# A decoder layer on one core: the last six pieces of the last gate through GpSimd's queue, the router bias beside the second output block

## The chip, the cores and the metric

The kernel runs on one core of a Trainium2 chip. The metric is the device time of one execution in microseconds (us). A core has TensorE (PE; its weight loads are PEld), VectorE (DVE), ScalarE (ACT) and GpSimd (POOL); SyncE (SP) here does little else than issue transfers. One set of 16 DMA engines moves all data between device memory and the core's own memory. An instruction stream runs strictly in its order on each engine, and an engine that waits holds up all that is behind it in its stream.

## The reference

The layer takes 256 tokens of width 2048, in float32. What matters here:

```python
ada = jax.nn.silu(c) @ w_ada[l] + b_ada[l]
sh1, sc1, gt1, sh2, sc2, gt2 = jnp.split(ada, 6, axis=-1)
h = modulate(rmsnorm(x, norm1_g[l]), sh1, sc1)
...                                              # input projection, attention, pooling
x = x + gt1[:, None, :] * (mix @ w_out[l])
h2 = modulate(rmsnorm(x, norm2_g[l]), sh2, sc2)
x = x + gt2[:, None, :] * hier_moe(h2, w_grp[l], w_exp[l], w1[l], w3[l], w2[l])
```

`hier_moe` picks one of 4 groups by the logits of `w_grp`, two of its 8 experts by those of `w_exp`, and adds the two experts' SwiGLU outputs, `(silu(h2 @ w1[e]) * (h2 @ w3[e])) @ w2[e]`, by their weights. The 32 experts' weights are 12 MB each and are all read.

## The kernel before

Three stages follow each other: the input projection with the vectors of the first sub-layer; attention, pooling and the output projection; the experts. Tile's scheduler decides at build time in which order each engine's instructions stand.

**Gates.** The vectors `gt1, sc2, sh2, gt2` are sums over 16 pieces of `w_ada` each. `ada_pieces` loads a piece (128x2048, 1 MB) into a slot through SP's queue (L177) and adds it, times `sT`, to an accumulator on VectorE (L178). `gt2` is section 5, the last; its accumulator lies in G6. From the second output projection on, the slots are the two halves of buffer G4 (tile `g4_70`) and buffer B8 (tiles `w_1976`, `w_1983` and so on), in turn. When all 16 pieces are in, `gate_end` sums over partitions by four products with `ones` (L290), each of which waits for the copy of the one ahead on ScalarE (L291).

**Second output projection and router.** `out_proj(mixA, ...)` (L613 products; L617, L618 on VectorE) goes through four blocks of 512 columns; its weights lie in G2 (`g2_68`) and G3 (`g3_69`). After each, `route_block` turns the block (L679, copies L681 and L682), forms router products (L686) with `h` in G7, sums squares (L690) and copies x for the gather (L693). `route_bias` (L670, 16 products, and the copy L672 into `brt`) stands after the third block. Then VectorE makes logits (L697, L708), the group and the two experts (L720 to L737), `memf`; products with `tri` and `ones` (L741 to L745) count tokens per expert; `pos` (L747) and the slot matrix `gq` (L784, L786) follow. `weights()` makes the combine weights `cmb`, and `most`, `mosti` (L767, L768), which SP loads into a register (L971) for the rare overflow path.

**Experts.** They go in eight quarters of 4 experts with 32 token slots each. `gather` builds `xg`: 64 products' worth of `x1c` by `gq` (L796), two groups of eight scalings (L800), a turn of the weights (L803) and its copy (L805). `hidden` goes through two halves of 1024 rows; in each, it takes the four `w1` tiles and then the four `w3` tiles of the quarter, 32 products each (L820); every tile is 2 MB (L815). A product shows as two records in the trace. All four tiles of such a block are read in turn, row group by row group, so each is free only near the block's end. `down` takes eight `w2` tiles (L856). Tiles go round a ring of buffers, G5, G1, G2, G3, G0, G7, G4, to which G6 comes when `gt2` is done. So the first `w3` block of the first quarter lies in G0, G7, G4 and G5 (second use), and the second half's `w1` in G1, G2, G3 and G0 (second use).

Of the kernel before, what the change touches and what calls it, by code (L numbers as in the profile page):

```python
# [12 lines left out]
ALU = mybir.AluOpType  # L13
AX = mybir.AxisListType.X
PSUM = bass.MemoryType.PSUM

P = 128
D = 2048
NT = 2
# [13 lines left out]
NE = 32  # L33
DE = 512
CAP = 32
RB = 8
RR = 4
QE = 4
# [41 lines left out]
def layer_kernel(ctx: ExitStack, tc: tile.TileContext, x, c, w_ada, b_ada, norm1_g, w_in, q_norm_g,  # L80
                 k_norm_g, w_pool, pool_scale, w_out, norm2_g, w_grp, w_exp, w1, w3, w2,
                 kconst, kband, out):
    nc = tc.nc
    x, out = x[0], out[0]
    w_ada, b_ada, w_in, w_out = w_ada[0], b_ada[0], w_in[0], w_out[0]
# [35 lines left out]
    def slot(shape, ring, key):  # L121
        t, at = turn(ring, key)
        if at is None:
            return one.tile(shape, F32, tag=t, name="w")
        return piece_of(t, at, shape)

    def bank(shape, tag):
        return ps1.tile(shape, F32, tag=tag, name=tag, bufs={"mm": 2, "sm": 1, "fl": 1}[tag])

    def banks(shape):  # L130
        return ps2.tile(shape, F32, tag="b2", name="b2")

    def t2(shape=(P, 512)):
        return rot.tile(list(shape), F32, tag="t2", name="t2", bufs=4)

    def r4(shape):
        return piece_of("G7", turn((0, 1024, 2048), "r4"), shape)
# [23 lines left out]
    ones = one.tile([P, P], F32, name="ones")  # L161
# [9 lines left out]
    nc.vector.tensor_copy(sT, pt[:, 0:16])  # L171


    def ada_pieces(sec, acc):
        def piece(k):
            w = slot([P, D], *fill_ring)
            nc.sync.dma_start(w, w_ada[k * P:(k + 1) * P, sec * D:(sec + 1) * D])  # L177
            nc.vector.scalar_tensor_tensor(acc, w, sT[:, k:k + 1], acc, op0=ALU.mult, op1=ALU.add)  # L178

        return [lambda k=k: piece(k) for k in range(KC)]  # L180
# [83 lines left out]
    for kq in range(4):  # L264
        pt = banks([P, 4, S])
        for i in range(NT):
            for j in range(4):
                k = kq * 4 + j
# [68 lines left out]
    def fill(n):  # L337
        for _ in range(n):
            step = next(steps, None)
            if step is not None:  # L340
                step()
                nsteps[0] += 1
# [331 lines left out]
    def route_block(n):  # L674
        xv = xs[:, :, n * 512:(n + 1) * 512].rearrange("p i (q r) -> p i r q", q=P, r=RR)
        pt = banks([P, 4, S])
        for i in range(NT):
            for u in range(4):
                nc.tensor.transpose(pt[:, u, i * P:(i + 1) * P], xv[:, i, u], ident)  # L679
        h = r4([P, 4, S])  # L680
        nc.scalar.copy(h[:, 0:2], pt[:, 0:2])  # L681
        nc.vector.tensor_copy(h[:, 2:4], pt[:, 2:4])  # L682
        pl = bank([P, NT, 36], "sm")
        for i in range(NT):
            for u in range(4):
                nc.tensor.matmul(pl[:, i], lhsT=h[:, u, i * P:(i + 1) * P], rhs=ws2[:, n * 4 + u],  # L686
                                 start=(u == 0), stop=(u == 3))
        for i in range(NT):
            t = t2()
            nc.scalar.activation(t, xs[:, i, n * 512:(n + 1) * 512], AF.Square, accum_out=ss2[:, i, n:n + 1])  # L690
        for i in range(NT):
            xc = xs[:, i, n * 512:(n + 1) * 512].rearrange("p (q r) -> p r q", r=RB)
            nc.scalar.copy(x1c[i][:, n // 2, :, (n % 2) * 64:(n % 2 + 1) * 64], xc)  # L693
        if n == 0:
            nc.vector.tensor_copy(lr, pl)
        else:
            nc.vector.tensor_add(lr, lr, pl)  # L697
        if n < 2:
            fill(9)
        if n == 2:  # L700
            route_bias()

    out_proj(mixA, 0, "wo_attn", route_block)
# [6 lines left out]
    def small(name, *shape):  # L710
        return one.tile([P, NT, *shape], F32, name=name)

    def bc(ap, *shape):
        return ap.to_broadcast([P, NT, *shape])
# [21 lines left out]
    memf = small("mem", NE)  # L736
    nc.vector.tensor_scalar(memf, lz, THRESH, None, op0=ALU.is_lt)  # L737


    pr = bank([P, 3, NE], "sm")  # L740
    nc.tensor.matmul(pr[:, 0], lhsT=tri, rhs=memf[:, 0], start=True, stop=True)  # L741
    nc.tensor.matmul(pr[:, 1], lhsT=ones, rhs=memf[:, 0], start=True, stop=False)
    nc.tensor.matmul(pr[:, 1], lhsT=tri, rhs=memf[:, 1], start=False, stop=True)
    nc.tensor.matmul(pr[:, 2], lhsT=ones, rhs=memf[:, 0], start=True, stop=False)
    nc.tensor.matmul(pr[:, 2], lhsT=ones, rhs=memf[:, 1], start=False, stop=True)  # L745
    pos = small("pos", NE)
    nc.vector.scalar_tensor_tensor(pos, pr[:, 0:2], 1.0, memf, op0=ALU.add, op1=ALU.mult)  # L747

    cmb, over = small("cmb", NE), small("over", NE)
    most = one.tile([P, 1], F32, name="most")  # L750
    mosti = one.tile([P, 1], I32, name="mosti")

    def weights():

        eg, sg, se = small("eg", NG), small("sg", 1), small("se", 1)
        nc.vector.tensor_sub(eg, lg, bc(mg, NG))
        nc.vector.tensor_sub(cmb, lm, bc(l8[:, :, 0:1], NE))
        nc.scalar.activation(eg, eg, AF.Exp)
        nc.scalar.activation(cmb, cmb, AF.Exp)
        nc.vector.tensor_mul(cmb, cmb, memf)  # L760
        nc.vector.reduce_sum(sg, eg, axis=AX)
        nc.vector.reduce_sum(se, cmb, axis=AX)
        nc.vector.tensor_mul(sg, sg, se)
        nc.vector.reciprocal(sg, sg)
        nc.vector.tensor_mul(cmb, cmb, bc(sg, NE))
        nc.vector.scalar_tensor_tensor(over, pr[:, 0:2], float(CAP), cmb, op0=ALU.is_ge, op1=ALU.mult)
        nc.vector.reduce_max(most, pr[:, 2], axis=AX)  # L767
        nc.vector.tensor_copy(mosti, most)  # L768


# [10 lines left out]
    def gather(e0):  # L781
        gq = rot.tile([P, NT, QE, CAP], F32, tag="gq", name="gq")
        gw = t2([P, NT, QE, CAP])
        nc.vector.tensor_tensor(gw, bc(iota[:, None, None, :], QE, CAP), bc(pos[:, :, e0:e0 + QE, None], QE, CAP), op=ALU.is_equal)  # L784
        for i in range(NT):
            nc.vector.tensor_scalar(gq[:, i], gw[:, i], rs2[:, i:i + 1], None, op0=ALU.mult)  # L786
        if e0 == 0:
            weights()
        nc.vector.tensor_mul(gw, gw, bc(cmb[:, :, e0:e0 + QE, None], QE, CAP))
        xg = one.tile([P, KC, QS], F32, tag="B8" if e0 // QE % 2 else "Pi", name="xg")  # L790
        for kq in range(2):
            px = banks([P, 8, QS])
            for u in range(8):
                k = kq * 8 + u
                for i in range(NT):
                    nc.tensor.matmul(px[:, u], lhsT=x1c[i][:, k // RB, k % RB],  # L796
                                     rhs=gq[:, i].rearrange("p e s -> p (e s)"), start=(i == 0), stop=(i == NT - 1))
            for u in range(8):
                k = kq * 8 + u
                nc.vector.tensor_scalar(xg[:, k], px[:, u], sc2T[:, k:k + 1], sh2T[:, k:k + 1], op0=ALU.mult, op1=ALU.add)  # L800
        pt = bank([P, NT, P], "sm")
        for i in range(NT):
            nc.tensor.transpose(pt[:, i], gw[:, i].rearrange("p e s -> p (e s)"), ident)  # L803
        gwT = rot.tile([P, NT, P], F32, tag="gwT", name="gwT")
        nc.vector.tensor_copy(gwT, pt)  # L805
        return xg, gwT
# [198 lines left out]
```

## Time and profile before

| | us |
|---|---|
| three runs | 1395.58, 1395.92, 1398.74 |
| median | 1395.92 |
| the profiled execution | 1393.28 |
| its span, first to last instruction | 1391.5 |
| TensorE busy | 1071.9 (77%) |
| VectorE busy | 447.1 (32%) |
| ScalarE busy | 100.0 (7%) |
| SP's queue (q1), share of 16 DMA engines' span | 97.9% |
| moved by DMA | 557.27 MB, mean 400 GB/s |

The profiled execution's own time is 1.78 us over its span. All times below count from the span's start. A row of a timeline gives start, length, engine, line, operation, output and inputs, count and, in brackets, how long the engine had been idle and what ended that. The granted clock is a share of 2.4 GHz.

### The profile page before, as it was taken

What the parts mean: (1) busy time and instruction counts of PE and PEld (TensorE: products, weight loads), DVE (VectorE), ACT (ScalarE), POOL (GpSimd) and SP (SyncE); (2) the same over time, 40 slices, a digit from 0 to 9 for tenths busy, and PEclk for the clock granted to TensorE, in tenths of its full rate; (3) what the DMA queues carried; (4) which work ended last, traced back from release to release, by engine and by line L of the source; (5) the groups of instructions that cost most, each with busy time, mean ns of one, the idle gap of its engine ahead of it and who ended that gap; (6) DMA issues with size and microseconds to landing.
All of it is one profiled execution on the core that took longest, in us unless ns stands there. A gap on an engine that the chain in (4) does not pass through costs nothing.

```text
span 1391.5 us, 12491 instructions
## 1 busy us (share of the span) xinstructions
PE 1071.9 (77%) x5227; PEld 433.6 (31%) x5227; DVE 447.1 (32%) x725; ACT 100.0 (7%) x225; POOL 9.1 (1%) x11
## 2 busy tenths in 40 slices
PE   4899998998997776677758767676776766777566
PEld 2455654544456231122213113121321311222112
DVE  1196667999677210201202111020220202012002
ACT  3200000424222000000000000000000000000000
POOL 1000000000000000000000000000000000000000
PEclk9999999999997979879979988997998998898789
DMA  9999998999999799999999999999999999999997
GB/s 320 328 385 385 400 386 324 342 361 322 400 365 405 325 427 428 427 428 427 427 429 428 428 429 426 427 428 428 428 429 427 428 427 427 428 429 428 429 424 283
DMA packets 101259, 557.27 MB, mean 400 GB/s; under 512 B 18792, under 2 KB 31056, under 8 KB 68688
## 3 DMA queue, kind: packets, MB, share of 16 engines
q1 hardware_dynamic: 97664, 554.22, 97.9%
q10 hardware_dynamic: 3472, 2.20, 0.5%
q8 instruction: 43, 0.70, 0.2%
q14 instruction: 16, 0.13, 0.0%
q0 software_dynamic: 64, 0.02, 0.0%
HBM read 554.31 MB, written 2.10 MB: 400 GB/s over the span
## 4 chain that ended last, share of the span: by engine, by line
DMA 52%; PE 33%; DVE 9%; issue 3%; SPq 2%; ACT 1%; ACTq 0%; DVEq 0%
DMA w<-in_w_dram 49%; PE mm L820 11%; PE mm L475 5%; PE mm L613 5%; PE b L861 4%; PE b L485 3%; DVE g L178 3%; DMA g<-in_w_in_dram 2%; DMA g<-in_w_ada_dram 1%; PE b L877 1%; DVE bacc L219 1%; SPq L815 1%; PE b L796 1%; DVE g L408 1%; DMA v8T<-in_b_ada_dram 1%
## 5 line engine op out<-in xcount | busy, mean ns | idle before, releaser
L820 PE MATMUL mm<-w,xg 128*32 128x512 f32 x2048 | 341.9, 704 | 162.8 <-DMA w<-in_w_dram 162.8
L861 PE MATMUL b<-w,t 128*32 128x512 f32 x896 | 178.0, 671 | 86.5 <-DMA w<-in_w_dram 81.0
L820 PEld LDWEIGHTS mm<-w,xg 128*32 128x32 f32 x2048 | 76.9, 126 | 415.1 <-DMA w<-in_w_dram 229.0
L800 DVE TENSOR_SCALAR xg<-b,sc2T,sh2T 128x128 f32<-128x128 f32 x128 | 42.3, 404 | 390.8 <-PE b L796 390.8
L475 PE MATMUL mm<-g,hT 128*128 128x512 f32 (+1 forms) x320 | 127.6, 553 | 12.0 <-DMA g<-in_w_in_dram 7.1
L178 DVE SCALAR_TENSOR_TENSOR g<-g,sT,g 128x2048 f32<-128x2048 f32 x52 | 122.0, 2346 | 12.2 <-DMA g<-in_w_ada_dram 12.1
L613 PE MATMUL mm<-g,mix 128*128 128x512 f32 x256 | 114.8, 601 | 4.2 <-DVE t L617 4.2
L861 PEld LDWEIGHTS b<-w,t 128*32 128x32 f32 x896 | 41.9, 116 | 217.6 <-DMA w<-in_w_dram 120.5
L841 DVE TENSOR_TENSOR t<-b,gt 128x512 f32<-128x512 f32 (+1 forms) x33 | 20.9, 671 | 273.0 <-PE b L861 250.7
L475 PEld LDWEIGHTS mm<-g,hT 128*128 128x128 f32 x320 | 57.2, 199 | 78.3 <-issue 64.2
L613 PEld LDWEIGHTS mm<-g,mix 128*128 128x128 f32 x256 | 48.2, 193 | 60.7 <-issue 55.1
L844 PE MATMUL mm<-t,gwT 128*128 128x512 f32 (+1 forms) x132 | 62.6, 605 | 3.3 <-DVE t L841 2.8
L796 PEld LDWEIGHTS b<-gq,x1c 128*128 128x128 f32 x512 | 59.8, 196 | 13.1 <-issue 6.7
L796 PE MATMUL b<-gq,x1c 128*128 128x128 f32 x512 | 62.7, 282 | 1.2 <-DVE gq L786 1.2
L824 ACT ACTIVATE t<-mm 128x512 f32<-128x512 f32 x8 | 4.8, 597 | 816.7 <-PE mm L820 816.7
L485 PE MATMUL b<-hT,g 128*128 128x256 f32 x256 | 56.9, 380 | 0.5 <-DMA g<-in_w_in_dram 0.4
L485 PEld LDWEIGHTS b<-hT,g 128*128 128x128 f32 x256 | 48.4, 190 | 11.2 <-issue 3.2
L846 DVE TENSOR_TENSOR xs<-xs,mm 128x512 f32<-128x512 f32 (+1 forms) x66 | 44.3, 671 | 17.7 <-PE mm L844 17.5
L825 DVE TENSOR_TENSOR t<-t,mm 128x512 f32<-128x512 f32 x8 | 5.5, 688 | 116.3 <-PE mm L820 116.3
L219 DVE SCALAR_TENSOR_TENSOR bacc<-g,sT,bacc 128x1024 f32<-128x1024 f32 x28 | 35.9, 1283 | 7.1 <-DMA g<-in_w_ada_dram 4.6
L844 PEld LDWEIGHTS mm<-t,gwT 128*128 128x128 f32 x132 | 21.2, 188 | 45.2 <-DVE xs L846 28.4
L178 DVE SCALAR_TENSOR_TENSOR g<-w,sT,g 128x2048 f32<-128x2048 f32 x12 | 28.1, 2346 | 2.3 <-DMA w<-in_w_ada_dram 2.2
(208 smaller groups left out, 514.4 us busy)
## 6 DMA issues: line engine op xcount, KB each, us to landing
w<-in_w_dram SPq DMA_DIRECT2D x190, 2048.0 KB, 21.3
g<-in_w_ada_dram SPq DMA_DIRECT2D x52, 1024.0 KB, 8.3
g<-in_w_ada_dram SPq DMA_DIRECT2D x44, 512.0 KB, 9.5
g<-in_w_in_dram SPq DMA_DIRECT2D x21, 1024.0 KB, 10.9
g<-in_w_out_dram SPq DMA_DIRECT2D x16, 1024.0 KB, 9.5
w<-in_w_ada_dram SPq DMA_DIRECT2D x12, 1024.0 KB, 7.4
w<-in_w_ada_dram SPq DMA_DIRECT2D x20, 512.0 KB, 9.7
g<-in_w_in_dram SPq DMA_DIRECT2D x14, 512.0 KB, 8.7
```

What stands on the lines that cost most here:

```text
L178: nc.vector.scalar_tensor_tensor(acc, w, sT[:, k:k + 1], acc, op0=ALU.mult, op1=ALU.add)
L219: nc.vector.scalar_tensor_tensor(acc, w[:, kk], sT[:, k:k + 1], acc, op0=ALU.mult, op1=ALU.add)
L475: nc.tensor.matmul(po[:, :width], lhsT=hcols(k0 + j, slice(i * P, (i + 1) * P)), rhs=w[:, j], start=(j == 0), stop=(j == nk - 1))
L485: nc.tensor.matmul(ppool[n][:, u], lhsT=w[:, j, u * P:(u + 1) * P], rhs=hcols(k, slice(0, S)), start=(k == 0 and u % 2 == 0), stop=(k == K ...
L613: nc.tensor.matmul(po, lhsT=mix[:, k, i * P:(i + 1) * P], rhs=ws[k // 4][:, k % 4], start=(k == 0), stop=(k == 7))
L796: nc.tensor.matmul(px[:, u], lhsT=x1c[i][:, k // RB, k % RB], rhs=gq[:, i].rearrange("p e s -> p (e s)"), start=(i == 0), stop=(i == NT - 1))
L800: nc.vector.tensor_scalar(xg[:, k], px[:, u], sc2T[:, k:k + 1], sh2T[:, k:k + 1], op0=ALU.mult, op1=ALU.add)
L820: nc.tensor.matmul(h[e * CAP:(e + 1) * CAP, :], lhsT=xg[:, k, e * CAP:(e + 1) * CAP], rhs=ws[e][:, r], start=(k == 0), stop=(k == KC - 1), ...
L841: nc.vector.tensor_mul(y[:, 0:m], py, gt2[:, c0:c0 + m])
L844: nc.tensor.matmul(pz[:, 0:m], lhsT=gwT[:, i], rhs=y[:, 0:m], start=True, stop=True)
L846: nc.vector.tensor_add(xv, xv, pz[:, 0:m])
L861: nc.tensor.matmul(py[n // 2][e * CAP:(e + 1) * CAP, (n % 2) * 512:(n % 2 + 1) * 512], lhsT=aT[:, f, e * CAP:(e + 1) * CAP], rhs=ws[e][:, ...
```

## The change

`gather(0)` puts a column of the first slot matrix `gq` on a list, `behind`. From then on a gate piece is loaded through GpSimd's queue, and ahead of each load VectorE copies that column into the piece's slot (L183), so that the load stands after it. At that point ten of the sixteen pieces of `gt2` have been made, and six are left. `route_bias` is called after the second block, not after the third. The two products for `most` (L744, L745 before) get a tile of their own and are formed in `weights()`, which with the product `gw * cmb` moves behind the gather's products in the program.

```diff
+    behind = []
     def ada_pieces(sec, acc):
         def piece(k):
             w = slot([P, D], *fill_ring)
-            nc.sync.dma_start(w, w_ada[k * P:(k + 1) * P, sec * D:(sec + 1) * D])
+            if not behind:
+                nc.sync.dma_start(w, w_ada[k * P:(k + 1) * P, sec * D:(sec + 1) * D])
+            else:
+                nc.vector.tensor_copy(w[:, 0:1], behind[0])
+                nc.gpsimd.dma_start(w, w_ada[k * P:(k + 1) * P, sec * D:(sec + 1) * D])
             nc.vector.scalar_tensor_tensor(acc, w, sT[:, k:k + 1], acc, op0=ALU.mult, op1=ALU.add)
...
-        if n == 2:
+        if n == 1:
             route_bias()
...
-    pr = bank([P, 3, NE], "sm")
+    pr = bank([P, NT, NE], "sm")
...
-    nc.tensor.matmul(pr[:, 2], lhsT=ones, rhs=memf[:, 0], start=True, stop=False)
-    nc.tensor.matmul(pr[:, 2], lhsT=ones, rhs=memf[:, 1], start=False, stop=True)
...
-        nc.vector.reduce_max(most, pr[:, 2], axis=AX)
+        pm = bank([P, NE], "fl")
+        nc.tensor.matmul(pm, lhsT=ones, rhs=memf[:, 0], start=True, stop=False)
+        nc.tensor.matmul(pm, lhsT=ones, rhs=memf[:, 1], start=False, stop=True)
+        nc.vector.reduce_max(most, pm, axis=AX)
...
         if e0 == 0:
-            weights()
-        nc.vector.tensor_mul(gw, gw, bc(cmb[:, :, e0:e0 + QE, None], QE, CAP))
+            behind.append(gq[:, 1, 0, 0:1])
...
+        if e0 == 0:
+            weights()
+        nc.vector.tensor_mul(gw, gw, bc(cmb[:, :, e0:e0 + QE, None], QE, CAP))
```

SP's stream at the start of the experts. Here `w_1998` and `w_1996` are the first half's last two `w1` tiles, `w_2032` to `w_2038` the first half's `w3` tiles of experts 0 to 3 (G0, G7, G4, G5), `w_2072` to `w_2076` the second half's `w1` tiles of experts 0 to 2 (G1, G2, G3), `w_2078` the one of expert 3 (G0), `w_2285` a `w2` tile in G6. Before:

```order
L177 DMA g4_70<-in_w_ada_dram 128x2048
L815 DMA w_2034<-in_w3_dram 128x4096
L177 DMA g4_70<-in_w_ada_dram 128x2048
L971 TENSOR_LOAD mosti_1897
L971 ISA x2
L815 DMA w_2036<-in_w3_dram 128x4096
L815 DMA w_2038<-in_w3_dram 128x4096
L815 DMA w_2072<-in_w1_dram 128x4096
L815 DMA w_2074<-in_w1_dram 128x4096
L815 DMA w_2076<-in_w1_dram 128x4096
L856 DMA w_2285<-in_w2_dram 128x4096
L815 DMA w_2078<-in_w1_dram 128x4096
```

The same place in SP's stream of the change, where 7 is added to most numbers: `w_2039`, `w_2041`, `w_2043`, `w_2045` are the first half's `w3` tiles of experts 0 to 3 (`w_2043` is the one in G4), `w_2079` to `w_2083` and `w_2085` the second half's `w1` tiles, `w_2292` the `w2` tile in G6:

```order
L825 DMA w_2041<-in_w3_dram 128x4096
L981 TENSOR_LOAD mosti_1895
L981 ISA x2
L825 DMA w_2045<-in_w3_dram 128x4096
L825 DMA w_2079<-in_w1_dram 128x4096
L825 DMA w_2081<-in_w1_dram 128x4096
L825 DMA w_2083<-in_w1_dram 128x4096
L825 DMA w_2043<-in_w3_dram 128x4096
L825 DMA w_2085<-in_w1_dram 128x4096
L825 DMA w_2119<-in_w3_dram 128x4096
L825 DMA w_2121<-in_w3_dram 128x4096
L825 DMA w_2123<-in_w3_dram 128x4096
```

The six gate pieces are gone from SP's stream, the load into G4 stood first of five behind the register load and now stands fifth, and the load into G6 stood sixth and now comes after the last row shown.

TensorE's stream where the first `w3` block begins (in the change, after the whole first `w1` block). `fl` tiles are the gate's final sums. Before:

```order
L820 MATMUL mm_1991<-w_2034,xg_1920 32x512
L290 MATMUL fl_2156<-g6_72,ones_94 128x512
L290 MATMUL fl_2159<-g6_72,ones_94 128x512
L290 MATMUL fl_2162<-g6_72,ones_94 128x512
L290 MATMUL fl_2165<-g6_72,ones_94 128x512
L820 MATMUL mm_1991<-w_2036,xg_1920 32x512
L820 MATMUL mm_1991<-w_2038,xg_1920 32x512
L820 MATMUL mm_1991<-w_2032,xg_1920 32x512
```

The same place in the change:

```order
L830 MATMUL mm_1998<-w_2039,xg_1901 32x512
L830 MATMUL mm_1998<-w_2041,xg_1901 32x512
L830 MATMUL mm_1997<-w_2079,xg_1901 32x512
L830 MATMUL mm_1997<-w_2081,xg_1901 32x512
L830 MATMUL mm_1997<-w_2083,xg_1901 32x512
L297 MATMUL fl_2163<-g6_72,ones_94 128x512
L297 MATMUL fl_2166<-g6_72,ones_94 128x512
L297 MATMUL fl_2169<-g6_72,ones_94 128x512
L830 MATMUL mm_1998<-w_2043,xg_1901 32x512
L830 MATMUL mm_1998<-w_2045,xg_1901 32x512
L830 MATMUL mm_1998<-w_2039,xg_1901 32x512
L830 MATMUL mm_1998<-w_2041,xg_1901 32x512
```

One product of each second-half `w1` tile and three of the gate's sums now stand ahead of the first product with `w_2043`; 30 of the block's 32 products stand behind that, and the last read of `w_2039`, whose buffer G0 the load of `w_2085` needs, is the 25th of them.

VectorE's stream from the slot matrix on, in the change (before, the six L178 rows stood one by one from the third output block on, and two of them between the router's steps):

```order
L794 TENSOR_SCALAR gq_1896<-t2_1897,rs2_1857 128x128 x2
L775 TENSOR_REDUCE most_1894<-fl_1966 128x1
L810 TENSOR_TENSOR t2_1897<-t2_1897,cmb_1892 128x256
L183 COPY w_1977<-gq_1896 128x1
L776 CAST mosti_1895<-most_1894 128x1
L183 COPY g4_70<-gq_1896 128x1 x2
L807 TENSOR_SCALAR xg_1901<-b2_1902,sc2T_1478,sh2T_1651 128x128 x8
L185 SCALAR_TENSOR_TENSOR g6_72<-w_1977,sT_102,g6_72 128x2048
L807 TENSOR_SCALAR xg_1901<-b2_1927,sc2T_1478,sh2T_1651 128x128 x8
L815 COPY gwT_1975<-sm_1972 128x256
L183 COPY w_1987<-gq_1896 128x1
L185 SCALAR_TENSOR_TENSOR g6_72<-g4_70,sT_102,g6_72 128x2048 x2
```

All six piece products stand behind the first group of scalings, and the last three pieces' copies come only after slots have been read.

## Rows read from the trace of the kernel before

**Rows 1.** Page, the chain that ended last, by line.

```profile
DMA w<-in_w_dram 49%; PE mm L820 11%; PE mm L475 5%; PE mm L613 5%; PE b L861 4%; PE b L485 3%; DVE g L178 3%; DMA g<-in_w_in_dram 2%; DMA g<-in_w_ada_dram 1%; PE b L877 1%; DVE bacc L219 1%; SPq L815 1%; PE b L796 1%; DVE g L408 1%; DMA v8T<-in_b_ada_dram 1%
```

**Rows 2.** Stretches: length, busy by engine, TensorE's granted clock, DMA share, GB/s.

```profile
429.00:440.00 11.00, 6.85 (x32) 6.59 (x31) 6.15 (x19) 2.43 (x4) 0.00 (x0) 0.50 1.01 430
...
452.60:460.60 8.00, 8.00 (x75) 3.72 (x75) 7.26 (x17) 0.00 (x0) 0.00 (x0) 1.00 0.05 20
462.00:470.00 8.00, 5.97 (x14) 1.33 (x10) 0.00 (x0) 2.34 (x4) 0.00 (x0) 1.00 0.99 422
500.00:1350.00 850.00, 610.34 (x3412) 187.97 (x3404) 113.06 (x242) 6.06 (x9) 0.00 (x0) 0.86 1.01 428
```

**Rows 3.** Timeline of SP's queue, 420 to 515 us.

```profile
441.02 0.33 SPq L177 DMA_DIRECT2D g<-in_w_ada_dram  x1
459.79 4.89 SPq L815 DMA_DIRECT2D w<-in_w_dram  x5
```

**Rows 4.** Line L815 from 455 to 470 us: five loads, issue to landing.

```profile
DMA to landing us min/median/max: 7.9/18.3/24.8
```

**Rows 5.** Timeline of VectorE, 425 to 460 us.

```profile
428.46 0.69 DVE L682 COPY g<-b 128x512 f32<-128x512 f32 x1 [1.11 <-ACT g L681]
...
451.18 2.64 DVE L800 TENSOR_SCALAR xg<-b,sc2T,sh2T 128x128 f32<-128x128 f32 x8 [0.37 <-PE b L796]
...
457.09 0.42 DVE L805 COPY gwT<-sm 128x256 f32<-128x256 f32 x1
457.42 2.35 DVE L178 SCALAR_TENSOR_TENSOR g<-g,sT,g 128x2048 f32<-128x2048 f32 x1
```

**Rows 6.** The chain in order of time: start, length, what; 422 to 446 us.

```profile
423.19 2.34 DVE g L178
425.53 0.61 DVE xs L618
...
432.64 3.61 PE sm L686 x16
...
438.75 2.25 DVE g L178
...
443.50 0.43 PE sm L744 x2
...
444.75 0.10 DVE most L767
```

**Rows 7.** Timeline of TensorE, 409 to 436 us.

```profile
411.13 1.42 PE L686 MATMUL sm<-ws,g 128*128 128x36 f32 x12
...
416.37 6.17 PE L613 MATMUL mm<-g,mix 128*128 128x512 f32 x14
...
426.77 5.48 PE L670 MATMUL sm<-wr,sh2T 128*128 128x36 f32 x32
```

**Rows 8.** Timeline of TensorE, 445 to 526 us.

```profile
445.56 8.94 PE L796 MATMUL b<-gq,x1c 128*128 128x128 f32 x64 [1.20 <-DVE gq L786]
...
454.64 7.94 PE L820 MATMUL mm<-w,xg 128*32 128x512 f32 x68
462.51 1.13 PE L290 MATMUL fl<-g,ones 128*128 128x512 f32 x2
464.31 1.12 PE L290 MATMUL fl<-g,ones 128*128 128x512 f32 x2 [0.68 <-ACT gt L291]
...
472.65 8.76 PE L820 MATMUL mm<-w,xg 128*32 128x512 f32 x60 [2.63 <-DMA w<-in_w_dram]
...
498.66 9.39 PE L820 MATMUL mm<-w,xg 128*32 128x512 f32 x60 [7.88 <-DMA w<-in_w_dram]
...
518.23 7.05 PE L820 MATMUL mm<-w,xg 128*32 128x512 f32 x58 [0.47 <-DMA w<-in_w_dram]
```

**Rows 9.** GpSimd's timeline, and VectorE's, at 333 us.

```profile
333.44 2.34 DVE L178 SCALAR_TENSOR_TENSOR g<-g,sT,g 128x2048 f32<-128x2048 f32 x1
...
333.70 0.49 POOL L283 DMA_DIRECT2D g<-in_b_ada_dram  x1 [0.30 <-POOL g L281]
```

More of the change, by code (lines that the diff above doesn't have):

```diff
@@ L743, in layer_kernel @@
     nc.tensor.matmul(pr[:, 1], lhsT=tri, rhs=memf[:, 1], start=False, stop=True)
-    nc.tensor.matmul(pr[:, 2], lhsT=ones, rhs=memf[:, 0], start=True, stop=False)
-    nc.tensor.matmul(pr[:, 2], lhsT=ones, rhs=memf[:, 1], start=False, stop=True)
     pos = small("pos", NE)
-    nc.vector.scalar_tensor_tensor(pos, pr[:, 0:2], 1.0, memf, op0=ALU.add, op1=ALU.mult)
+    nc.vector.scalar_tensor_tensor(pos, pr, 1.0, memf, op0=ALU.add, op1=ALU.mult)
     cmb, over = small("cmb", NE), small("over", NE)
@@ L765, in weights @@
         nc.vector.tensor_mul(cmb, cmb, bc(sg, NE))
-        nc.vector.scalar_tensor_tensor(over, pr[:, 0:2], float(CAP), cmb, op0=ALU.is_ge, op1=ALU.mult)
-        nc.vector.reduce_max(most, pr[:, 2], axis=AX)
+        nc.vector.scalar_tensor_tensor(over, pr, float(CAP), cmb, op0=ALU.is_ge, op1=ALU.mult)
+        pm = bank([P, NE], "fl")
+        nc.tensor.matmul(pm, lhsT=ones, rhs=memf[:, 0], start=True, stop=False)
+        nc.tensor.matmul(pm, lhsT=ones, rhs=memf[:, 1], start=False, stop=True)
+        nc.vector.reduce_max(most, pm, axis=AX)
         nc.vector.tensor_copy(mosti, most)
```

## The prediction

> **What bounds the kernel now.** I read the chain that ended last first: half of it is waiting for weight transfers [rows 1]. The stretches say how hard the DMA engines work: from 500 to 1350 us they move 428 GB/s without a pause [rows 2]. At that rate a 2 MB weight tile takes 4.9 us and a 1 MB gate piece 2.45 us, and whatever the engines compute in the expert stage is hidden behind it. So the time is set by how many bytes are in when the expert stage begins, that is, by how long the DMA engines stand still around 410 to 500 us. They do in one place: 452.6 to 460.6 us, share 0.05 [rows 2]. SP's queue says why: after the last gate piece (441.02) nothing is issued until 459.79 [rows 3]. The load that stands next in SP's stream goes into G4, which the last piece product on VectorE, 457.42 to 459.77 [rows 5], still reads. Five loads then go out, the first lands 7.9 us later [rows 4], of which 4.9 are its bytes and 3.0 the way there and the notice; and from 462 us on the transfers never stop again [rows 2]. TensorE goes on in the first `w3` block at 472.65 and, after the seventh load, at 498.66 [rows 8]. That last row is my mark: the six loads ahead had landed 4.9 us earlier, at 493.8.
>
> **The change part by part.** *The way to the slot matrix gets shorter.* On it now stand a piece product between the two-expert search and its next step, 2.25 us; the two pairs of `most` products, 0.43 each; and the `most` reduction, 0.10 [rows 6]. All leave it: 3.2 us. The router bias moves into the last dense block. Its 32 records took 5.48 us; twelve records of like products between dense ones took 1.42, or 0.119 each [rows 7], so there it costs 32 x 0.119 = 3.8 us. The dense products, which ended at 416.37 + 6.17 = 422.5 [rows 7], end at 426.3. No piece product (2.34 us) now stands between the two VectorE steps of 0.6 to 0.7 us that follow [rows 6], so x is done at 427.7, where it was at 426.1 [rows 6]. From there to the end of the second copy took 428.46 + 0.69 - 426.14 = 3.0 us [rows 5, 6]; the eight router products of the block before, now ahead, add some 0.3: 431.0. The last 16 records take 1.9 us at 0.119 or 3.6 as measured [rows 6], so they end at 432.9 to 434.6; they ended at 436.2. Gain 1.6 to 3.3; I take 2.4. Together 5.6 us, bounds 4.8 to 6.5: the gather, which began at 445.56 [rows 8], begins at 440.0.
>
> *The first block.* From the gather's start to the first expert product it was 9.1 us, and 68 records took 7.94 [rows 8]. The 64 records of the first `w1` block thus run from 449.1 to 456.6; its tiles are last read in its last four products, about 0.7 us from the end. At 455.9 SP's four reloads go out; the register load ahead of them waits for `mosti`, which is ready soon after the gather starts, so it costs nothing. Their bytes begin some 1.4 us later, at 457.3 (half of the 3.0).
>
> *The gate pieces.* SP no longer carries them. The idle stretch moves rather than goes: pieces one to three are issued at about 441 and are through by 451. Piece four needs a slot back. The first scalings start 451.18 - 445.56 = 5.6 us after the gather [rows 5, 8]; scalings 2.64, piece product 2.35, scalings 2.64, and a copy of about 0.4 [rows 5] follow: issued at 453.7, through at about 457.6. Pieces five and six come two piece products later, at 458.5, with the reloads. The six slot copies are one column each and cost nothing beside those. What GpSimd needs to issue 1 MB is in no row: 0.33 us is SP's issue [rows 3], 0.49 GpSimd's for 8 KB [rows 9]. I take 0.5; the lower end changes nothing, and the upper end is the length of one VectorE instruction, 2.35 us, by which piece four would fall among the reloads: +2.45.
>
> The row at 333.70 shows GpSimd's issue done in 0.49 us while a piece product of 2.34 us ran on VectorE [rows 9]. The Trainium skill, SBUF — State Buffer, "SBUF: two separate sides", has a rule against this change: GpSimd cannot write the descriptors of its transfers while VectorE runs a two-port operation such as a float32 copy, and the transfer waits for its end. By the row, 0.5 us stands; by the rule the sum would be 2.45 higher, if a two-port operation lay there. No run here shows one beside a large transfer of this queue.
>
> *The load into G4 comes last.* This is the term that decides. In SP's stream four reloads stand ahead of it. Bytes from 457.3: four reloads 19.6, pieces five and six 4.9, a rest of piece four 0.3, and its own 4.9 make 487.0; it lands 1.6 later, at 488.6. (It must be in the queue by 481. If both queues share the engines, piece six lands near 472, and its product ends by 476.) Before, G4 came first, the block began when the second of five had landed, and three loads, 14.7 us, were under way meanwhile. Now all seven buffers are full when it lands, and SP's next load, into G0, waits for a block that has hardly begun. The load into G6, which filled that place before, stands behind it. TensorE passes the fourth reload at 483.7, then three gate sums (two steps of 1.8, one of 1.13 [rows 8], 4.8 with a product ahead 5.3), so it starts on the block at 489.0. G0 is free after 25 of 30 products, 50 of 60 records. Sixty took 8.76 at 472.65 and 9.39 at 498.66, 58 took 7.05 at 518.23 [rows 8]: 50 take 6.1 to 7.8; I take 7.3. At 496.3 G0's load goes out, alone, and lands 7.9 later: 504.2. The DMA engines stand still for about 10.5 us.
>
> *Sum.* 504.2 against 493.8 with the same bytes moved: **+10.4 us**. From there on both keep the queue full (four loads, 19.6 us, follow G0's at once, and the next block takes under 10). The output's end is untouched. The profiled execution took 1393.28, so 1403.7; it lies 2.64 under the median of the three runs, 1395.92, and in that measure I forecast **1406.3**. Bounds: the gather 0.9 earlier, the block 1.2 shorter and the gather at 0.119 a record (7.6 for 8.94, so 1.3) give +7.0; the gather 0.8 later, the block 0.5 longer and piece four among the reloads (2.45) give +14.2.
>
> **The rivals.** *The gate ends late.* If GpSimd's transfers do not share but stand behind the four reloads, piece six is through at 457.3 + 24.8 = 482.1 and lands at 483.7, its product ends at 486.1, and G4's load, alone, lands at 494.0, 5.4 later than above: +15.8, 1411.7. For it: the DMA engines are already full there, and no row shows two large queues at once. Against: the slack is 5 us. The Trainium skill, DMA: Bandwidth & Descriptors, "SWDGE vs HWDGE vs iDMA", says that an engine goes round-robin between its queues, which speaks against this rival; no row here tests it.
>
> *The early start pays.* The other side, not slower: TensorE keeps 2.4 GHz, where the granted clock was 0.50 around the router [rows 2], and the pieces finish early. Its point is whether piece six is through before the reloads begin at 455.9. Then pieces five and six fall out of the 488.6 (-4.9), the clock gives the lower bound's 3.4, and the time is +10.4 - 8.3 = +2.1, or 1398.0. For it: the idle stretch is long enough for six pieces. Against: five steps of VectorE between 440 and 458 set when slots come free, and the order fixes them. *No hole at all* would need G4's load to land with others under way; then G0's lands at 488.6 + 4.9 = 493.5, no change, and a further gain would have to come from the idle stretch. The stream of SP excludes it unless I misread whose buffer is whose.
>
> **How the numbers follow.** Forecast 0.67; late gate 0.16; early start or no hole, 0.13 within 0.3%, and 0.04 for a gain that I cannot name. 0.3% (4.2 us) is about what a measurement of this kernel can tell from no change. So slower 0.83, same 0.13, faster 0.04. The forecast's own range is +7.0 to +14.2, 1402.9 to 1410.1; with the late gate up to 1411.7, and a little on either side for the spread of the runs before (1395.58 to 1398.74), I give 1401 to 1413, which leaves out the last two cases.
>
> **What would show it.** Right: the gather's first product near 440, the first expert product near 449, the four reloads near 456 in SP's queue, G4's load fifth, landing near 489; then a stretch of 9 to 12 us near 487 to 498 with almost no DMA, and TensorE resuming with the second half's `w1` near 504. The old gap at 452.6 to 460.6 is a shorter one near 451 to 457. Wrong: no idle stretch after G4's load, or a G4 load issued ahead of the reloads; a gather later than 442 would say that the bias cost more in the dense block than 3.8 us.

## The result

| | before | after |
|---|---|---|
| median of four runs, us | 1395.75 (1393.81 to 1398.74) | 1411.43 (1409.20 to 1413.33) |
| the profiled execution | 1393.28 | 1410.86 |
| its span | 1391.5 | 1409.1 |
| mean moved by DMA, GB/s | 400 | 395 |

The change is slower: ratio 1.0106, 95% interval 1.009 to 1.0122, which is 12.6 to 17.0 us. The forecast was 1406.3, with a range of 1401 to 1413; the time lies inside, 5.1 us above the forecast. Two single executions of the experiments below, 2798.52 us of the gate part alone and 5171.23 us of the pieces in halves, are left out; with them these two kernels' medians would be 1419.06 and 1396.83.

The two traces are 3.3 us apart before anything changes: ten records of dense products that the change leaves alone start at 419.67, after 416.37 [rows 7]. Half of it is there when the dense products of the first output projection begin (277.24, after 275.73). Nearly all of the rest comes in 22 records of dense products, which took 11.36 us from 392.78, at a granted clock of 0.82, where they took 9.71 at 1.00 before. The run on SP's queue and the one with four pieces left, described below, have the change's edits and 9.71 there; the run with free buffers on SP's queue has 11.24. So I take the 3.3 for chance from run to run, though no run shows what brings it. So "less the 3.3" below means a time of after on before's scale.

TensorE of after, the rows that answer to [rows 7, 8] (7 was added to most line numbers, so L820 is L830):

```profile
419.67 4.46 PE L620 MATMUL mm<-g,mix 128*128 128x512 f32 x10
423.97 3.66 PE L677 MATMUL sm<-wr,sh2T 128*128 128x36 f32 x32
...
442.98 9.47 PE L803 MATMUL b<-gq,x1c 128*128 128x128 f32 x64 [0.25 <-DVE gq L794]
...
452.60 7.92 PE L830 MATMUL mm<-w,xg 128*32 128x512 f32 x68
477.44 1.88 PE L830 MATMUL mm<-w,xg 128*32 128x512 f32 x2 [16.93 <-DMA w<-in_w_dram]
...
488.38 1.92 PE L830 MATMUL mm<-w,xg 128*32 128x512 f32 x2 [2.97 <-DMA w<-in_w_dram]
490.23 1.84 PE L297 MATMUL fl<-g,ones 128*128 128x512 f32 x2
...
495.60 7.06 PE L830 MATMUL mm<-w,xg 128*32 128x512 f32 x60
...
509.71 9.96 PE L830 MATMUL mm<-w,xg 128*32 128x512 f32 x60 [6.00 <-DMA w<-in_w_dram]
```

The early part is faster, as planned: the gather starts at 442.98, 439.7 less the 3.3, where it was 445.56 [rows 8]. Then TensorE has next to nothing to do from 460 to 488 us, runs the first `w3` block at 495.60 without a wait inside it, and has only one gate sum until 509.71. The chain that ended last passes through exactly these pieces:

```profile
459.80 0.23 SPq L825
...
461.07 27.26 DMA w<-in_w_dram
...
495.67 6.19 PE mm L830 x56
501.86 7.81 DMA w<-in_w_dram
```

It goes from SP's four reloads to the landing of the fourth, through the gate's sums into the block, and from the block's 56th record to G0's load, which goes out alone. Where transfers are missing is best read from stretches that cover the whole of the difference (length, busy by engine, granted clock, DMA share, GB/s). After:

```profile
400.00:420.00 20.00, 20.00 (x71) 10.93 (x70) 16.36 (x13) 4.23 (x8) 0.00 (x0) 1.00 0.79 292
420.00:430.00 10.00, 10.00 (x54) 6.79 (x52) 5.69 (x6) 2.21 (x4) 0.00 (x0) 1.00 0.55 211
430.00:450.00 20.00, 14.94 (x89) 14.36 (x89) 9.03 (x48) 5.45 (x9) 1.60 (x3) 0.66 0.96 388
450.00:460.00 10.00, 10.00 (x92) 4.64 (x91) 9.96 (x19) 0.00 (x0) 0.53 (x1) 1.00 0.55 210
460.00:490.00 30.00, 5.94 (x10) 0.54 (x6) 10.13 (x10) 0.00 (x0) 1.05 (x2) 0.57 1.01 428
490.00:510.00 20.00, 12.65 (x73) 3.55 (x76) 0.00 (x0) 2.35 (x4) 0.00 (x0) 0.93 0.41 161
```

The same of before:

```profile
400.00:420.00 20.00, 20.00 (x71) 10.93 (x71) 18.28 (x14) 5.60 (x10) 0.00 (x0) 1.00 0.86 320
420.00:430.00 10.00, 8.53 (x53) 6.98 (x51) 6.40 (x9) 4.32 (x9) 0.00 (x0) 0.92 1.00 397
430.00:450.00 20.00, 12.60 (x63) 12.24 (x63) 14.32 (x41) 1.71 (x3) 0.00 (x0) 0.53 1.00 426
450.00:460.00 10.00, 10.00 (x95) 6.21 (x97) 8.92 (x20) 0.00 (x0) 0.00 (x0) 1.00 0.29 117
460.00:490.00 30.00, 18.92 (x97) 4.37 (x86) 1.01 (x4) 2.34 (x4) 0.00 (x0) 0.88 0.98 409
490.00:510.00 20.00, 12.12 (x79) 4.25 (x79) 0.00 (x0) 1.85 (x2) 0.00 (x0) 0.66 1.01 428
```

Take the difference of the last columns, times the length, over 428 GB/s, the full rate [rows 2]. After loses 1.3 us in 400 to 420, 4.3 in 420 to 430 (the pieces that filled this stretch are gone, and SP's next loads waited 13.4 us for dense products, that is, for buffers), 1.8 in 430 to 450, and **12.5 in 490 to 510**. It gains 2.2 in 450 to 460 and 1.3 in 460 to 490. Together 16.4 us of transfer time; the spans differ by 17.6.

### The profile page after: what moved, and what is told of

The parts are those of the page before. It is cut to its first block, busy times and chain, and to the rows that moved or that the text cites. A ratio compares the mean times of both kernels' runs of the same rounds, so it can differ in the third digit from the quotient of the medians.

```text
span 1409.1 us, 12506 instructions
## 1 busy us (share of the span) xinstructions
PE 1077.8 (76%) x5227; PEld 433.4 (31%) x5227; DVE 447.9 (32%) x731; ACT 100.1 (7%) x225; POOL 12.3 (1%) x17
## 4 chain that ended last, share of the span: by engine, by line
DMA 52%; PE 34%; DVE 7%; issue 3%; SPq 2%; ACT 1%; ACTq 0%; DVEq 0%
DMA w<-in_w_dram 49%; PE mm L830 11%; PE mm L482 6%; PE mm L620 5%; PE b L871 3%; PE b L492 2%; DVE g L185 2%; DMA g<-in_w_in_dram 2%; DMA g<-in_w_ada_dram 1%; SPq L825 1%; PE b L803 1%; DVE bacc L226 1%; DVE g L415 1%; DMA v8T<-in_b_ada_dram 1%; PE mm L854 1%
## 5 line engine op out<-in xcount | busy, mean ns | idle before, releaser
L830 PE MATMUL mm<-w,xg 128*32 128x512 f32 x2048 | 340.5, 697 | 179.3 <-DMA w<-in_w_dram 179.3
L871 PE MATMUL b<-w,t 128*32 128x512 f32 x896 | 184.6, 697 | 84.9 <-DMA w<-in_w_dram 79.4
L830 PEld LDWEIGHTS mm<-w,xg 128*32 128x32 f32 x2048 | 76.3, 125 | 429.9 <-DMA w<-in_w_dram 229.5
L856 DVE TENSOR_TENSOR xs<-xs,mm 128x512 f32<-128x512 f32 (+1 forms) x66 | 44.2, 671 | 17.7 <-PE mm L854 17.5
```

The source lines that it names most:

```text
L830: nc.tensor.matmul(h[e * CAP:(e + 1) * CAP, :], lhsT=xg[:, k, e * CAP:(e + 1) * CAP], rhs=ws[e][:, r], start=(k == 0), stop=(k == KC - 1), ...
L856: nc.vector.tensor_add(xv, xv, pz[:, 0:m])
L871: nc.tensor.matmul(py[n // 2][e * CAP:(e + 1) * CAP, (n % 2) * 512:(n % 2 + 1) * 512], lhsT=aT[:, f, e * CAP:(e + 1) * CAP], rhs=ws[e][:, ...
```

## A measure that fits every run

The same can be done once for the whole first part. Stretch from 0 to 530 us, before and then after:

```profile
0.00:530.00 530.00, 461.07 (x1847) 249.87 (x1847) 331.69 (x486) 95.84 (x218) 9.06 (x11) 0.95 0.97 366
```

```profile
0.00:530.00 530.00, 453.65 (x1777) 246.77 (x1777) 330.00 (x487) 95.92 (x218) 12.25 (x17) 0.93 0.94 352
```

Before lost 530 x (1 - 366/428) = 76.8 us there, after 94.1. For every kernel of this study the span less this loss comes to 1313 to 1316 us:

| kernel (described below) | GB/s to 530 us | lost, us | span, us | span less lost |
|---|---|---|---|---|
| before | 366 | 76.8 | 1391.5 | 1314.7 |
| after | 352 | 94.1 | 1409.1 | 1315.0 |
| gate part alone | 345 | 102.8 | 1416.5 | 1313.7 |
| without the gate part | 364 | 79.3 | 1394.0 | 1314.7 |
| free buffers, GpSimd's queue | 365 | 78.0 | 1393.1 | 1315.1 |
| the change on SP's queue | 352 | 94.1 | 1408.1 | 1314.0 |
| free buffers, SP's queue | 366 | 76.8 | 1390.3 | 1313.5 |
| gate part alone, free buffers | 363 | 80.5 | 1396.6 | 1316.1 |
| before, free buffers | 367 | 75.5 | 1389.7 | 1314.2 |
| four pieces left | 359 | 85.4 | 1400.4 | 1315.0 |
| bias part, free buffers | 369 | 73.1 | 1387.2 | 1314.1 |
| pieces in halves | 365 | 78.0 | 1393.0 | 1315.0 |

A unit of GB/s is 1.2 us here, so these agree within rounding and a little. In part this is bookkeeping: all of them move the same 557.3 MB, and each ran at 428 GB/s from 530 to 1350 us, so what is lost ahead of that has to come out at the end. That they do run so, and that the end takes each the same time, is what the table shows; it doesn't tell why the engines stood still. The prediction's first step, that the time is set by how long the DMA engines stand still around the start of the experts, holds for twelve kernels that differ by 29 us.

## The experiments

The kernel before ran beside each set: 1396.51 us (median of 23) beside the first four runs, 1397.25 (28) beside the next four, 1397.47 (17) beside the last two. "Theory 1" in the quoted texts is the forecast's (G4's load behind the four reloads); the others are named in them.

**The gate part alone.** The kernel before with the list `behind`, the slot copies and GpSimd's queue; bias, `most` and `weights()` as before:

```diff
+            if not behind:
+                nc.sync.dma_start(w, w_ada[...])
+            else:
+                nc.vector.tensor_copy(w[:, 0:1], behind[0])
+                nc.gpsimd.dma_start(w, w_ada[...])
...
+            behind.append(gq[:, 1, 0, 0:1])
```

> The kernel before with the gate pieces alone changed: the last six go through GpSimd's queue behind the slot matrix; router bias, token counts and combine weights stay as they were. SP's stream has the load into G4 fifth behind four reloads, as in the change. Theory 1 (the load into G4 comes last and the DMA engines run dry): as slow as the change or a little slower, since the bias stays on the way to the slot matrix: +13 to +19 us over the kernel before, with a stretch of 9 to 12 us of almost no DMA after that load. Theory 2 (the loss comes from the bias products in the dense block, which hold back the loads into G2 and G0): within 4 us of the kernel before. Theory 3 (GpSimd's queue is slow in itself): as theory 1 in time, without a dry stretch after G4's load.

Measured 1418.39, ratio 1.0149 (1.0122 to 1.0175), some 22 us slower, 3 us more than the top of theory 1's range. The loss is all in the gate part, and is larger than that of the whole change. TensorE there:

```profile
444.76 10.11 PE L804 MATMUL b<-gq,x1c 128*128 128x128 f32 x64 [1.20 <-DVE gq L793]
...
494.09 2.08 PE L297 MATMUL fl<-g,ones 128*128 128x512 f32 x2
...
501.59 8.77 PE L828 MATMUL mm<-w,xg 128*32 128x512 f32 x60
...
517.73 2.79 PE L828 MATMUL mm<-w,xg 128*32 128x512 f32 x12 [6.31 <-DMA w<-in_w_dram]
```

The picture of after, later by 1.8 us at the gather, 6.0 at the block and 8.0 at the landing of G0's load. Of the 6.0, 3.9 are there when the fourth reload is passed (492.24) and 2.1 come from the gate's sums, which ran at a granted clock of 0.50. So it was not the bias that cost the time.

**Without the gate part.** The change with nothing put on the list `behind`, so that all pieces stay on SP's queue, without copies:

```diff
-            behind.append(gq[:, 1, 0, 0:1])
+            pass
```

> The change without its gate part: bias after the second block, token counts and weights moved, all sixteen pieces in SP's stream as before. G4's load then stands third of five, behind two reloads and ahead of two. Theory 1: no dry stretch behind that load; the router gains 2 to 3 us, the idle stretch near 452 to 460 stays as it depends on the last piece: -4 to +2 us against the kernel before. Theory 2: +10 to +16 us. Theory 3: as theory 1.

Measured 1395.99, ratio 1.0002 (0.9988 to 1.0016): no difference. The bias takes 3.66 us in the dense block here too, but little of it arrives at the gather (445.63, or 444.2 on the scale of before, where it was 445.56), since piece products on VectorE stand between the router's steps again:

```profile
443.08 0.60 PE L748 MATMUL sm<-mem,kc 128*128 128x32 f32 x2 [9.15 <-DVE mem L744]
```

In after TensorE waited 3.68 us at this place. The bias move needs the gate part: it shortens the path only once the late pieces are out of the router's way. The gate part doesn't need the bias move for that: alone it brought the gather to 444.76, 441.6 on the scale of before.

**The change with free buffers.** Theory 1 says that it matters whose buffers the late pieces hold, and not when they come or by which queue. So they were given buffers that no early expert load needs (B8, which two of the six had before, is one of them):

```diff
-            w = slot([P, D], *fill_ring)
+            w = slot([P, D], *(([("G6", 0), ("B8", None), ("gate", None)], "behind") if behind else fill_ring))
```

> The change with other slots for the six late pieces: the free half of G6, B8 and the buffer of the first gate, in place of the halves of G4 and B8. Nothing else differs; the pieces still go through GpSimd's queue behind the slot matrix. G4 is then free for its weight tile as soon as the tenth piece is used, and SP's stream has that load among the first, ahead of the register load. Theory 1: no dry stretch after the first w3 block; the seventh load after the reloads' begin lands near 488.6 where the kernel before has it at 493.8: -5 us, between -8 and -1, against the kernel before, and some 16 to 20 us under the change. Theory 2: +10 to +16 us, as the change. Theory 3: +5 us or more, since the pieces are as late as in the change.

Measured 1393.68, ratio 0.9979 (0.9968 to 0.999): 2.8 us under the kernel before (theory 1 had 5, between 1 and 8) and 17.7 under the change, with one line. Its block and the stretches that were empty:

```profile
470.90 8.62 PE L830 MATMUL mm<-w,xg 128*32 128x512 f32 x60 [10.90 <-DMA w<-in_w_dram]
...
495.43 8.29 PE L830 MATMUL mm<-w,xg 128*32 128x512 f32 x60
```

```profile
490.00:500.00 10.00, 9.32 (x37) 2.21 (x40) 0.00 (x0) 1.17 (x2) 0.00 (x0) 0.60 1.00 426
500.00:510.00 10.00, 10.00 (x69) 5.27 (x62) 0.00 (x0) 2.94 (x4) 0.00 (x0) 1.00 1.01 428
```

The gate's sums are as late as in after (two of the four stand ahead of the products at 495.43, the last ends at 508.5, where after had it at 503.7), the last piece's product starts at 480.45 (481.49 in after), and no transfer waits: G4's load went out ahead of the four reloads, so the first `w3` block runs from 470.90 and frees its four buffers in time. This is the run that shows the cause.

**The change on SP's queue.** `nc.gpsimd.dma_start` becomes `nc.sync.dma_start`, so pieces five and six stand behind the four reloads in one queue. This is the mechanism of the rival "the gate ends late".

> The change with the six late pieces on SP's queue in place of GpSimd's, still behind the slot matrix and with the same slots. In SP's stream pieces five and six now stand behind the four reloads and ahead of the load into G4. Theory 1: the rival of the prediction in which the gate ends late, for sure: piece six lands after the reloads, its product ends near 486, G4's load goes out alone: 3 to 8 us slower than the change, +18 to +24 us over the kernel before. Theory 3: faster than the change, +0 to +10 us. Theory 2: as the change, +12 to +17 us.

Measured 1411.22, ratio 1.0117 (1.0095 to 1.014), 14.7 us slower: as much as the change, and less than I expected of it. SP's timeline and TensorE's:

```profile
454.92 2.06 SPq L825 DMA_DIRECT2D w<-in_w_dram  x4
457.08 0.93 SPq L184 DMA_DIRECT2D g<-in_w_ada_dram  x2
486.34 16.79 SPq L825 DMA_DIRECT2D w<-in_w_dram  x5
```

```profile
478.95 1.91 PE L830 MATMUL mm<-w,xg 128*32 128x512 f32 x2 [2.98 <-DMA w<-in_w_dram]
486.37 2.08 PE L297 MATMUL fl<-g,ones 128*128 128x512 f32 x2 [5.51 <-DVE g L185]
...
493.95 8.11 PE L830 MATMUL mm<-w,xg 128*32 128x512 f32 x60
```

The rival's figures are here: G4's load goes out alone at 486.34 (the rival's sum had 486.1), the block starts at 493.95 (494.0), and the time is 14.7 over the kernel before (15.8); 0.4 is to be added to the first two for the scale of before. I had added this loss to that of the change. It takes its place: with the pieces behind them the reloads land earlier, and most of what G4's late load costs is saved there. This trace came early at the dense products (415.98, 3.7 before after's); counted from there its fourth reload is passed 5.7 us earlier than in after and its block starts 2 us later. The times don't tell the two apart.

**Free buffers, SP's queue.** The two edits together.

> The late pieces in free buffers (as in the run with those slots, 1393.7 us), but on SP's queue. Theory 1 (what counts is whose buffer the pieces hold: G4's load, free of them, stands ahead of the reloads): the queue is of no account, the three late pieces stand in SP's stream near the four reloads and cost their bytes either way: 1393.7, between 1391 and 1397. Rival (it is GpSimd's queue, which lets the transfers share with SP's, that gives the gain once the slots are free): piece four's wait for its slot near 457 holds SP's stream, all reloads go out 2 to 4 us later, 1396 to 1400.

Measured 1392.00, ratio 0.997 (0.9958 to 0.9982). Inside the range of theory 1, 1.7 us under the run on GpSimd's queue. GpSimd's queue gives nothing here; whether it costs that 1.7 stays open, as the two intervals overlap.

**The gate part alone, with free buffers.** The first run with the line of the third.

> Only the gate part of the change, with the late pieces in free buffers; router bias and the products for most stand as in the kernel before. The same gate part with the slots of G4 and B8 took 1419.1. Theory 1: the stretch without transfers after 500 us goes, as G4's load is no longer last; the gather starts 2 to 3 us later than with the bias move: 1396, between 1393 and 1399. Rival (the gate part costs by itself, for its transfers run beside the reloads, and the bias move made good for some of it): 1403 or more.

Measured 1396.08, ratio 0.9993 (0.998 to 1.0005), as theory 1 had it. The 22 us are gone by that one line: the largest single effect of the study, and on a kernel without the bias move.

**The kernel before, with free buffers.** Nothing of the change; only the last six pieces' buffers (the scheduler then moves some piece products too, and none stands between the router's last steps):

```diff
-            w = slot([P, D], *fill_ring)
+            w = slot([P, D], *(([("G6", 0), ("B8", None), ("gate", None)], "behind") if sec == 5 and k >= 10 else fill_ring))
```

> The kernel before with one edit: the last six pieces of the last gate go into free buffers instead of G4 and B8; SP's queue, no copies, bias as before. Theory 1: G4's load goes out as soon as piece ten's product has read it, in the stretch of 8 us that stood nearly empty at 452.6 to 460.6, so about one load (4.9 us) is won: 1391, between 1388 and 1395. Rival (the stretch is set by the first w1 block's end, when slots come free, and the pieces now put into SP's stream later keep it as long): 1395 to 1397.

Measured 1390.91, ratio 0.9963 (0.9953 to 0.9973), 6.3 us faster. Its stretches:

```profile
450.00:460.00 10.00, 10.00 (x86) 7.21 (x88) 7.27 (x17) 0.00 (x0) 0.00 (x0) 0.93 1.01 424
460.00:470.00 10.00, 6.36 (x42) 1.62 (x34) 6.38 (x8) 1.17 (x2) 0.00 (x0) 1.00 0.64 242
```

The stretch that was nearly empty [rows 2] is full, and a shorter one of about 4 us is left at 460 to 464, where all seven buffers wait for the first block to end. The two traces show less than the medians: the spans differ by 1.8 us and the lost time by 1.3. The profiled execution of before was 4 us faster than this set's median, so the traces bear out only a part of the 6.3.

**Four pieces left instead of six.** The change with `fill(10)` for `fill(9)` after the first two output blocks. G4's load still stands fifth.

> The change with one number: ten pieces instead of nine are loaded beside each of the first two output blocks, so four are left for GpSimd's queue, not six. G4's load still stands fifth, behind the four reloads, but the load into G6 comes ahead of the one into G0. Theory 1: no piece's bytes stand among the reloads (4.9 us less), the gate sums come earlier, G4's load lands near 484 to 486, and the stretch without transfers shrinks to some 5 to 7 us: 1403, between 1400 and 1407. Rival (the dose does not matter, G4's load must wait for the block before in any case): 1409 to 1412. Rival (the order of G6's load alone closes the stretch): 1396 to 1399.

Measured 1402.45, ratio 1.0042 (1.0028 to 1.0057), 5.2 us slower: about a third of the change's loss. TensorE:

```profile
488.82 10.04 PE L830 MATMUL mm<-w,xg 128*32 128x512 f32 x60 [2.99 <-DMA w<-in_w_dram]
505.76 8.40 PE L830 MATMUL mm<-w,xg 128*32 128x512 f32 x60 [6.91 <-DMA w<-in_w_dram]
```

Counted from the dense products (418.09 here) the block starts 5.2 us earlier than in after; it waits for G4's load itself, no longer for gate sums, which were done in the idle time before it. The load was in at 488.8, 487.1 on the scale of before, 1 to 3 us later than I expected. The hole is there still, shorter, since it comes from the place of that load.

**The bias part, with free buffers.** The run without the gate part, with the line for the buffers from the run on the kernel before: SP's queue, no slot copies, bias beside the second block.

> The change without its gate part (bias move and products for most only), with the last six pieces in free buffers, on SP's queue with no copies. The two edits won 0 (that run: 1396.0) and 6 us (the kernel before with free buffers: 1390.9) apart. Theory 1 (time is what the DMA engines lose; the earlier gather moves the reloads forward by 2 to 3 us once the stretch without transfers is set by the first block's end): 1388.5, between 1386 and 1391. Rival (the earlier dense block end is given back on VectorE, where late piece products stand between the router's steps, as without the gate part): 1391 to 1395.

Measured 1389.01, ratio 0.9941 (0.9925 to 0.9956), 8.5 us faster than before and the fastest of all. The reloads of the kernel before with free buffers, and of this one:

```profile
463.27 17.75 SPq L815 DMA_DIRECT2D w<-in_w_dram  x8
460.37 17.79 SPq L825 DMA_DIRECT2D w<-in_w_dram  x8
```

They go out 2.9 us earlier, as theory 1 had it. With the buffers right, an earlier gather is worth something: 1.9 us beside the kernel before with free buffers (1390.91, another set), where it was worth nothing alone; the two intervals just touch, so its size is not well known.

**Pieces in halves.** The third run with each late piece loaded as two halves of 1024 columns, to see what sets the share that GpSimd's queue gets beside SP's.

> The run with free buffers on GpSimd's queue (1393.7), each late piece loaded as two halves of 1024 columns, so its rows are 4 KB instead of 8 KB, beside SP's rows of 16 KB. There, pieces five and six landed 7.4 us apart, 1.05 MB at a third of the engines. Theory A (the engines take one packet from either queue in turn, whatever its size): the share falls to 4 of 20, a fifth, pieces five and six land about 12 us apart; the time rises by 0 to 5 us, as the gate sums come later. Theory B (the share is set by bytes or by a limit of GpSimd's queue, not by packets): 7 to 8 us apart as before.

Measured 1396.59, ratio 1.0001 (0.9988 to 1.0014), 2.9 us over the run it is compared with. Transfers by queue, with packets, MB and share of the engines' time, while both queues are busy. After, 466 to 478 us, with rows of 8 KB in q0, GpSimd's:

```profile
q1 hardware_dynamic: 234, 3.31, 64.4%
q0 software_dynamic: 235, 1.79, 35.3%
```

The halves, 466 to 490 us, with rows of 4 KB:

```profile
q1 hardware_dynamic: 563, 8.19, 80.1%
q0 software_dynamic: 562, 2.04, 21.0%
```

Packet for packet in turn, so the bytes go as the packets' sizes do: a third and a fifth. Theory A holds by the counts. The edit does more than cut the loads in two: the copied column lies in a piece's first half, so nothing holds the second half behind the slot matrix, and three halves went out before it, at 388.79, 419.59 and 427.99, the others from 440.31 on:

```profile
419.59 0.53 POOL L185 DMA_DIRECT2D w<-in_w_ada_dram  x1 [30.26 <-DVE g L186]
```

So the halves stand in another order, and the time of this run is no test of the share. Pieces five and six came 5.8 us apart and not 12 (their products start at 487.99 and 493.80); 12.7 lie between four and five. From the fourth to the sixth, 475.26 to 493.80, three halves landed, 6.2 us each: at 0.52 MB that is a fifth of 428 GB/s, which fits the counts.

## Why the prediction was right

**What bounds the kernel**: shown, by the table of twelve spans, with what was said there on bookkeeping.

**The way to the slot matrix**: 3.66 us for the bias where 3.8 was taken, the gather at 439.7 for 440.0, the first block at 449.3 for 449.1, the reloads at 456.5 for 455.9 (all less the 3.3). GpSimd's timeline:

```profile
457.29 0.53 POOL L184 DMA_DIRECT2D w<-in_w_ada_dram  x1 [11.46 <-DVE w L183]
462.00 1.05 POOL L184 DMA_DIRECT2D g<-in_w_ada_dram  x2 [4.18 <-DVE g L183]
```

Piece four goes out at 454.0 less the 3.3 (453.7), pieces five and six at 458.7 (458.5), each issue takes 0.53 (0.5), the one at 457.29 while a piece product ran on VectorE. The upper bound of 2.45 for that was not needed. The Trainium skill's rule for it (SBUF — State Buffer, "SBUF: two separate sides") is one for two-port operations such as a float32 copy; it doesn't name a product of this kind among them, and in no run shown here does a large copy run beside a large issue, so the rule is not tested.

**The load into G4 comes last**: the mechanism is shown, by the chain, by the hole and by the runs with free buffers, in which the program changes in nothing but the pieces' buffers, and SP's order follows from that. Three of its terms were off. VectorE's rows tell of the first, SP's row of G4's load and two stretches (length, busy by engine, granted clock, DMA share, GB/s) of the others:

```profile
473.75 2.35 DVE L185 SCALAR_TENSOR_TENSOR g<-g,sT,g 128x2048 f32<-128x2048 f32 x1 [8.93 <-DMA g<-in_w_ada_dram]
481.49 2.35 DVE L185 SCALAR_TENSOR_TENSOR g<-g,sT,g 128x2048 f32<-128x2048 f32 x1 [5.39 <-DMA g<-in_w_ada_dram]
```

```profile
483.87 0.33 SPq L825 DMA_DIRECT2D w<-in_w_dram  x1
```

```profile
488.40:490.20 1.80, 1.80 (x2) 0.16 (x2) 0.00 (x0) 0.00 (x0) 0.00 (x0) 0.50 1.02 437
495.70:501.90 6.20, 6.20 (x58) 1.85 (x60) 0.00 (x0) 0.59 (x1) 0.00 (x0) 1.00 0.01 3
```

- *Piece six* could be used at 478.2 less the 3.3, where it was to land near 472: I had shared the engines by halves, and the queue got a third. Its product ended at 480.5, not by 476, and the term's own limit was 481. The five microseconds of slack were half a microsecond, so it was luck that G4's load still went out behind bytes under way, and that the forecast's mechanism held rather than the late gate.
- *The start on the block* came at 492.3 and not at 489.0. It was the gate's sums that it waited for: G4's load took 9.3 us and was in at 489.9 (488.6). The fourth reload was passed at 485.1 for 483.7; its one product took 1.85 us at a granted clock of 0.50, the 1.2 GHz to which TensorE fell while it waited, where I took 0.5; the three sums took 5.4 for 4.8.
- *The block* freed G0 after 6.2 us and not 7.3, by two errors that go against each other. TensorE was back at 2.4 GHz by then (granted clock 1.00), 0.11 us a record, where I took 0.146. And the load went out behind the 56th record, not the 50th, that is, behind the 28th product of the 30 and not the 25th: with four tiles read in turn, the last read of G0's tile is among the last four. The chain of before has 56 at the same place too (7.94 us from 472.65).
- *G0's load* took 7.85 from issue to landing, as taken (7.9).

So 504.2 + 3.3 - 1.1 = 506.4, which is 509.71 less the 3.3: +12.6 us at the mark, where +10.4 was forecast, and inside the forecast's own range (+7.0 to +14.2). The hole of 12.5 us in 490 to 510 was forecast at 9 to 12. The spans are 1.7 us further apart than the mark (17.6 less 15.9). The medians are 15.7 apart, 3.1 more than the 12.6: of the 5.1 us between forecast and time the terms explain 2.2, and the rest I can't place; the interval of the ratio begins at 12.6.

**The rivals.** The late gate gave 1411.7, nearly the time measured, and yet it isn't what happened: the engines were full from 460 to 490, piece six was in 7 us ahead of the fourth reload (481.0 and 488.3), and G4's load went out at the end of piece six's product, 483.87, still behind bytes under way. Who goes by the number alone would have picked the wrong cause; the run on SP's queue shows what that cause looks like. The Trainium skill, DMA: Bandwidth & Descriptors, "SWDGE vs HWDGE vs iDMA", had an engine go round-robin between its queues, which the prediction named against this rival: the trace agrees, 235 packets to 234. *The early start pays* fell by its own condition: four pieces had been issued by the time the reloads began, not six, and only three had landed. *No hole at all* did not come, as SP's stream said; the free buffers show that this case was one line away.

**What the prediction left out** is the other side of the move. The pieces taken from 420 to 450 us left a hole of 6.1 us there. It wasn't needed for the sum, which started from the reloads; a sum of lost transfer time needs it.

## What to carry to other kernels

When a kernel is bound by transfers, sum the time that the DMA engines stand still: it accounted for every span here to within about 3 us, and it tells at once whether a faster start was paid back later. Before moving a load later, ask whose buffer it lands in and which load stands behind that buffer in the queue; here six loads of 1 MB went through G4 and B8, and taking them out of G4 was worth 6 to 22 us by the medians, where the queue and an earlier gather were worth 2 us or less. A time that matches a rival's number is not its mechanism: look for the idle engines that the rival needs.

## What I had not expected of the hardware

- GpSimd's queue and SP's take turns by packet: 235 to 234 with 8 KB and 16 KB rows, 562 to 563 with 4 KB and 16 KB. So smaller rows mean a smaller share, a third and a fifth, and of two loads of 1 MB issued together at 462.0 beside loads of 2 MB one could be used at 473.75, the other at 481.49, where the first of five loads of 2 MB landed after 7.9 [rows 4].
- A single product after a wait of 3 to 17 us took 1.88 to 1.92 us for its two records, at a granted clock of 0.50; the 56 records of the block, right after the gate's sums, took 6.19, or 0.11 each.
